# Gated and merged blocks kept on chip in the merge of a hybrid layer, x's first half loaded behind them, and longer loads in the planner's model

## The chip, the cores and the metric

The kernel runs on one core of one Trainium2 chip. The metric is the device time of one execution in microseconds (us). Three runs of the kernel before took 2212.59, 2214.92 and 2218.59 us; the median is 2214.92 us.

The core has five engines that work side by side, each on its own list of instructions in order: TensorE (PE, matrix multiplication, with its weight loads shown as PEld), VectorE (DVE), ScalarE (ACT), GpSimd (POOL) and SyncE (SP). Nearly every DMA of this kernel is issued from SP's list, so an issue that has to wait holds up every issue behind it. SBUF is the memory on the chip that the engines compute from, PSUM holds the results of matmuls until an engine reads ("evicts") them, and DRAM is outside.

## What is computed

One layer of a sequence model over 1024 positions with 1024 channels. Two branches (a gated delta rule and a gated linear attention) are computed, each is projected, and the two are merged by sigmoid gates and projected once more; then come cross attention and an MLP.

```python
y_a = o_a.reshape(bsz, seq, GDN_WIDTH) @ w_branch_gdn[i].astype(dt)
...
y_b = o_b.reshape(bsz, seq, GLA_VAL_WIDTH) @ w_branch_gla[i].astype(dt)
merged = jax.nn.sigmoid(gate_a) * y_a + jax.nn.sigmoid(gate_b) * y_b
x = x + merged @ w_out[i].astype(dt)
```

The change is in these lines: what happens to the gated `y_b` and to the merged blocks between the matmuls.

## The kernel before, in words

**Precision and tiles.** All activations are kept with the channel on the 128 partitions: a block is 128 channels by 512 positions (`HALF`), 256 KB; D = 1024 gives 8 blocks of two halves. Every float32 matrix is split in a high and a low part (`split`: ScalarE copies the rounded high part, L574, VectorE or GpSimd subtracts it from the original for the low part, L575), and a product is three matmuls (`mm3`: high by high L534, high by low L536, low by high L538).

**Seven products.** The projections use a Strassen-Winograd scheme (`wino`): one pair of output blocks (index `u`) needs seven products p = 0 to 6 instead of eight, each of four steps of three matmuls, so 12 matmuls of 512 columns. The weights for the products are sums of the raw weights (L1634 to L1639, which the planner may give to VectorE or to GpSimd), split afterwards into `wop` tiles; the raw weights are in a ring of four buffers (`RAWS`), two for each `u`. The operands of the seven products are loaded from DRAM through small staging tiles (`e` and `rawa`) and split into seven slots named A1a, A1b, B0a, B0b, B1a, B1b and t4. Each product is evicted by VectorE additions in `sums` (L1681); a block of the output is final after p = 1, 4, 5 or 6, and `done` is then called for it.

**The merge** (`phase_merge`, L1761 to L1854). It does 4 passes of `wino` with two `u` each: "yb" for the pairs (0, 1) and (2, 3), then "ya" for the same pairs. Each pass is 7 products by 2 `u` by 12 = 168 matmuls, 672 in all.

- In yb, each final half block is gated by one VectorE instruction (L1792: tanh part plus 1, times the block) and stored to DRAM tiles `m1d` (L1793): 16 stores.
- In ya, each final half block is gated (L1823), the gated half block of yb is loaded back from `m1d` and added (L1824). For the first pair the sum goes to the DRAM tiles `md` (L1829, 8 stores) and is loaded back when slots for it are free, through the staging tiles. The merged blocks are then split (`put`): high parts into B0a and B1a, low parts into B0b and B1b, for the first and second half of the positions.
- The gates come through a ring of eight half blocks in the slot A0b (`fetcher`), loaded from `tgd`; in ya the ring carries the gates and `m1d` in turn. The ring of ya is a new tile in the same slot: its first load waits until VectorE has read the last gate of yb.
- The slot A0a takes the first half of x at the start of ya, and A0b the second half at the end; `phase_out` adds x to the output projection there (L1891). `phase_out` starts its first matmuls with the merged blocks 0 to 4 and 6, then 5 and 7, of the first half.

**What sets the order.** The kernel is traced once without an order. A planner (`Plan`) reads the instructions, gives each one a cost, works out what depends on what, gives every instruction other than a matmul a latest start from the matmuls that need it (`latest`), and runs a list scheduler four times (`forward`); the best order is then fixed for every engine. The same pass decides which of the free sums go to GpSimd. A load counts in the model as landing a fixed time after its issue plus its bytes over a rate, 2050 ns and 390 bytes per ns. Any change of these numbers can therefore move instructions anywhere in the program. Buffers are given out in a ring: a load waits until the last reader of the tile that had its buffer is done.

## Time and profile before

One execution was profiled; it took 2218.4 us, its span from the first to the last instruction is 2216.6 us. It is one execution, 3.5 us above the median of the three runs, so differences are worked out within it and then taken from the median.

| what | value |
|---|---|
| median of three runs | 2214.92 us |
| profiled execution, span | 2218.4 us, 2216.6 us |
| TensorE busy | 2160.5 us, 97% of the span |
| VectorE busy | 1702.1 us, 77% |
| ScalarE busy | 1092.8 us, 49% |
| GpSimd busy | 208.2 us, 9% |
| mean granted TensorE clock | 0.991 of full |
| moved by DMA | 300.20 MB |

How to read it: a busy share is an average over stages with different limits, so the stage that the change touches has to be looked at by itself, with the stretches of time that the windows view gives. Rows of the timeline give the start, the duration, the engine, the line, the output and the inputs, and in brackets how long the engine had been idle and what released it. Matmuls overlap: a row of a matmul lasts 0.39 us at full clock though the next one starts 0.23 us later, and a VectorE row of 0.68 us is followed by the next after 0.60 us.

### The profile page before, as it was taken

The page shows a single profiled execution, that of the slowest core. Times are in us where ns is not written, and L with a number is a line of the kernel's source. Part 1 is how long each engine was busy: PE and PEld are TensorE (multiplying, and loading weights), DVE is VectorE, ACT ScalarE, POOL GpSimd, SP SyncE. Part 2 cuts the span into 40 slices and gives each one's busy share as a digit, 9 for nine tenths or more (in the row PEclk, how much of TensorE's full clock was granted, in tenths as well). Part 3 has the DMA queues.
Part 4 walks back from the last instruction along what each step waited for, and adds up shares of the span by engine and source line. Part 5 has one row for each costly group of instructions (what it writes and reads, how often), then busy time and mean ns, then how long its engine had stood idle before and what let it go on. Part 6 is the DMA issues. An engine that isn't in the chain of part 4 may idle for free.

```text
span 2216.6 us, 32151 instructions
## 1 busy us (share of the span) xinstructions
PE 2160.5 (97%) x11504; PEld 1835.2 (83%) x11504; DVE 1702.1 (77%) x3161; ACT 1092.8 (49%) x2215; POOL 208.2 (9%) x242
## 2 busy tenths in 40 slices
PE   8899999999999999999999999999999999999996
PEld 8788878988889888888878778998788888887876
DVE  7776997778796978969689965479989777567666
ACT  5544555354455545555544343465655555433433
POOL 0000000010220323222110000000100000000001
PEclk9999999999999999999999999999999999999998
DMA  8842122121311112112177841255354445687752
GB/s 273 273 153 73 59 101 86 57 83 49 120 38 50 65 47 74 48 35 76 40 248 256 285 175 67 77 168 184 116 184 142 152 157 182 212 265 249 239 175 84
DMA packets 147311, 300.20 MB, mean 135 GB/s; under 512 B 15688, under 2 KB 22216, under 8 KB 147152
## 3 DMA queue, kind: packets, MB, share of 16 engines
q1 hardware_dynamic: 140352, 289.75, 39.5%
q10 hardware_dynamic: 6800, 8.42, 1.1%
q8 instruction: 90, 1.47, 0.3%
q14 instruction: 69, 0.57, 0.1%
HBM read 212.35 MB, written 85.75 MB: 134 GB/s over the span
## 4 chain that ended last, share of the span: by engine, by line
PE 71%; DMA 11%; DVE 11%; ACT 2%; issue 2%; SPq 1%; POOL 0%; DVEq 0%; ACTq 0%; POOLq 0%
PE pd L538 18%; PE pd L534 18%; PE pd L536 18%; DMA raw<-in_w_dram 3%; PE ps L534 2%; PE ps L538 2%; PE ps L536 2%; DVE wop L575 2%; PE ps L606 1%; DMA e<-ad 1%; PE ps L1327 1%; DMA Gd<-gst 1%; SPq L503 1%; DMA A0b<-tgd 1%; DMA rawa<-pd 1%
## 5 line engine op out<-in xcount | busy, mean ns | idle before, releaser
L574 ACT ACTIVATE wop<-raw 128x512 fp32r<-128x512 f32 (+1 forms) x472 | 312.6, 669 | 377.1 <-PE pd L538 174.6
L575 DVE TENSOR_TENSOR wop<-raw,wop 128x512 fp32r<-128x512 f32 (+1 forms) x435 | 309.6, 713 | 79.4 <-ACT wop L574 77.4
L1185 DVE SCALAR_TENSOR_TENSOR acc<-pd,convw,acc 128x511 f32<-128x511 f32 x144 | 106.8, 742 | 15.7 <-ACT acc L1182 15.5
L538 PE MATMUL pd<-t,wop 128*128 128x512 f32 x268 | 107.9, 402 | 0.1
L534 PE MATMUL pd<-t,wop 128*128 128x512 f32 x268 | 106.0, 395 | 1.3 <-ACT wop L574 1.3
L536 PE MATMUL pd<-t,wop 128*128 128x512 f32 x268 | 105.1, 392 | 0.0
L534 PE MATMUL pd<-B1a,wop 128*128 128x512 f32 (+1 forms) x220 | 82.9, 377 | 0.3 <-ACT wop L574 0.3
L538 PE MATMUL pd<-B1a,wop 128*128 128x512 f32 (+1 forms) x220 | 82.8, 376 | 0.1
L538 PE MATMUL pd<-A1a,wop 128*128 128x512 f32 x180 | 73.5, 409 | 2.3 <-DVE wop L575 2.3
L534 PE MATMUL pd<-A1a,wop 128*128 128x512 f32 x180 | 72.4, 402 | 2.7 <-DVE u L1723 2.0
L536 PE MATMUL pd<-A1a,wop 128*128 128x512 f32 x180 | 71.7, 399 | 0.0
L574 ACT ACTIVATE whi<-raw 128x512 fp32r<-128x512 f32 x70 | 42.0, 626 | 55.3 <-PE pd L536 50.1
L536 PE MATMUL pd<-B0b,wop 128*128 128x512 f32 x172 | 67.6, 393 | 0.9 <-DVE B0b L575 0.9
L534 PE MATMUL pd<-A1b,wop 128*128 128x512 f32 x144 | 57.8, 402 | 3.3 <-DVE u L1723 3.3
L534 PEld LDWEIGHTS pd<-t,wop 128*128 128x128 f32 x268 | 50.4, 188 | 12.7 <-ACT wop L574 2.0
L538 PEld LDWEIGHTS pd<-t,wop 128*128 128x128 f32 x268 | 50.4, 188 | 12.6 <-DVE wop L575 1.0
L536 PEld LDWEIGHTS pd<-t,wop 128*128 128x128 f32 x268 | 50.4, 188 | 11.6
L538 PE MATMUL pd<-A1b,wop 128*128 128x512 f32 x144 | 57.5, 399 | 0.1
L536 PE MATMUL pd<-B1a,wop 128*128 128x512 f32 (+1 forms) x156 | 57.3, 367 | 0.0
L536 PE MATMUL pd<-A1b,wop 128*128 128x512 f32 x144 | 56.9, 395 | 0.0
L534 PE MATMUL pd<-A0a,whi 128*128 128x512 f32 x140 | 55.6, 397 | 0.8 <-ACT whi L574 0.8
L538 PE MATMUL pd<-A1a,wlo 128*128 128x512 f32 x140 | 56.3, 402 | 0.0
(603 smaller groups left out, 6996.4 us busy)
## 6 DMA issues: line engine op xcount, KB each, us to landing
raw<-in_w_dram SPq DMA_DIRECT2D x120, 256.0 KB, 3.9
raw<-in_w_gdn_dram SPq DMA_DIRECT2D x64, 256.0 KB, 2.8
raw<-in_w_dram SPq DMA_DIRECT2D x32, 512.0 KB, 4.4
e<-ad SPq DMA_DIRECT2D x63, 256.0 KB, 4.7
ad<-q SPq DMA_DIRECT2D x45, 256.0 KB, 2.6
rawa<-ad SPq DMA_DIRECT2D x42, 256.0 KB, 4.6
A0b<-tgd SPq DMA_DIRECT2D x32, 256.0 KB, 4.9
ad<-acc SPq DMA_DIRECT2D x30, 256.0 KB, 2.3
```

The lines of the kernel that those rows point to most:

```text
L503: self.nc.sync.dma_start(dst, src)
L534: nc.tensor.matmul(out, lh, rh, start=first and i == 0, stop=False)
L536: nc.tensor.matmul(out, lh, rl, start=False, stop=False)
L538: nc.tensor.matmul(out, ll, rh, start=False, stop=last and i == n - 1)
L574: nc.scalar.activation(hi, raw, AF.Copy)
L575: (lo_eng or nc.gpsimd).tensor_tensor(lo, raw, hi.bitcast(F32), SUB)
L606: self.nc.tensor.transpose(pt[:, i * P:(i + 1) * P], s, self.ident)
L1185: nc.vector.scalar_tensor_tensor(x, pt[:, 0:HALF - d], tap, x, MUL, ADD)
L1327: nc.tensor.matmul(pt[0:96, i * n:(i + 1) * n], PF[:, v + i, 0:96], Z, start=True, stop=True)
```

## The change

1. The gated blocks of yb are no longer stored. L1792 writes its result into a tile on chip: blocks 0 to 3 in the slot A0a, blocks 4 to 7 in a new tile `m` of the same size in a pool of its own. In ya the ring carries only gates (16 loads instead of 32), and L1824 reads the block on chip. For the first pair the merged sum is written over the gated block in A0a, and `put` splits from there; the stores to `md` and the loads from it are gone.
2. Since A0a is taken, x's first half is loaded after the splits of the second half of the first pair's blocks are issued (after p = 3 of the last pass).
3. In the planner's model a load takes 2600 ns plus its bytes at 300 bytes per ns. The cost of a ScalarE instruction with a second output and of one with a broken access pattern, and that of narrow matmuls, are changed too.
4. The pool of `m` ends with the merge; the later phases are the same.

```diff
-ROUNDS, TOP, PAD, WINDOW, LOAD, HORIZON = 4, 228656, 128, 3413, 1283, 30000
+ROUNDS, TOP, PAD, WINDOW, LOAD, HORIZON, LAND, RATE = 4, 228656, 128, 3413, 1283, 30000, 2600, 300
...
-            self.dma, self.cost, self.own, self.lat = True, 60, 2050, 2050
+            self.dma, self.cost, self.own, self.lat = True, 60, LAND, LAND
...
-            elif m == 64:
+            elif max(m, size(ins_[1])) == 64:
...
-            self.cost, self.own, self.lat = d - 100 + (240 if psum(ins_[0]) else 385) * (len(outs) > 1), 130, 135
+            broken = any(len(x.ap) > 2 and any(st != x.ap[-1][0] * x.ap[-1][1] for st, _ in x.ap[-2:-1]) for x in ins_ + outs)
+            self.cost, self.own, self.lat = d - 100 + 240 * (len(outs) > 1) + 140 * broken, 130, 135
...
-                    last[j] = min(last[j], s - q.to(o, j in self.raw[i]) - q.bytes / 390)
+                    last[j] = min(last[j], s - q.to(o, j in self.raw[i]) - q.bytes / RATE)
...
-                e = free["ring"] = max(e, free["ring"]) + o.bytes / 390
+                e = free["ring"] = max(e, free["ring"]) + o.bytes / RATE
...
+        m = [self.slot("A0a", (4, T), F32), self.til(self.mp, [P, 4, T], "m")]
+        mb = lambda blk, half: m[blk // 4][:, blk % 4, hs(half)]
+
         def yb_done(u):
             def done(i, half, x):
-                nc.vector.scalar_tensor_tensor(x, get(), 1.0, x, ADD, MUL)
-                self.nc.sync.dma_start(self.m1d[2 * u + i][:, hs(half)], x)
+                nc.vector.scalar_tensor_tensor(mb(2 * u + i, half), get(), 1.0, x, ADD, MUL)
                 more()
             return done
...
-        x[0] = self.slot("A0a", (NB, HALF), F32)
-        srcs = []
-        for us in pairs:
-            for i, half in stages:
-                for u in us:
-                    srcs += [self.tgd[2 * u + i][:, hs(half)], self.m1d[2 * u + i][:, hs(half)]]
-        get, more = fetcher(srcs)
-        for k in range(0, NB, 2):
-            self.load(x[0][:, k:k + 2], a["xT"][:, k:k + 2, 0:HALF])
+        get, more = fetcher([self.tgd[2 * u + i][:, hs(half)] for us in pairs for i, half in stages for u in us])
+
+        def load_x(half):
+            x[half] = self.slot(("A0a", "A0b")[half], (NB, HALF), F32)
+            for k in range(0, NB, 2):
+                self.load(x[half][:, k:k + 2], a["xT"][:, k:k + 2, hs(half)])
...
             def done(i, half, c):
-                ta, m1 = get(), get()
-                nc.vector.scalar_tensor_tensor(c, ta, 1.0, c, ADD, MUL)
-                nc.vector.tensor_tensor(c, m1, c, ADD)
+                blk = 2 * u + i
+                nc.vector.scalar_tensor_tensor(c, get(), 1.0, c, ADD, MUL)
                 more()
-                more()
-                blk = 2 * u + i
-                if not last:
-                    nc.sync.dma_start(self.md[blk][:, half], c)
-                elif half in mT:
+                to = c if last else mb(blk, half)
+                nc.vector.tensor_tensor(to, mb(blk, half), c, ADD)
+                if last and half in mT:
                     put(blk, half, c)
-                else:
+                elif last:
                     held.append((blk, half, c))
             return done
...
-                        put(blk, half, self.staged(sp, self.md[blk][:, half]))
+                        put(blk, half, mb(blk, half))
+                    if half:
+                        load_x(0)
```

The planner makes a new order for the whole program from this. Three places of it are shown, as rows of one engine's list: line, operation, output and inputs with their numbers, and the shape. The numbers of tiles differ between the two kernels, and from L62 on a line of the change is a few lines off the line of before (L1682 is before's L1681, L1797 is L1792, L1824 is L1823, L1827 is L1824).

VectorE, near the start of yb's second pass, before. A `raw` tile is a half of one `u`'s raw weights; raw_11806 is the second half for the second `u`, and gets the buffer that raw_11322 had.

```order
L575 TENSOR_TENSOR wop_11636<-raw_11322,wop_11636 128x512
L1681 TENSOR_TENSOR q_11746<-ps_11809,q_11746 128x512
L575 TENSOR_TENSOR wop_11877<-raw_11801,wop_11877 128x512
L1635 TENSOR_TENSOR raw_11801<-raw_11801 128x4x128
L1634 TENSOR_TENSOR raw_11805<-raw_11805,raw_11806 128x4x128
```

The same place in the change, from the last reader of raw_11310, whose buffer raw_11795 gets, up to ten rows on; the first sum that reads raw_11795 (L1635 raw_11794<-raw_11794,raw_11795) comes after four more rows.

```order
L576 TENSOR_TENSOR wop_11629<-raw_11310,wop_11629 128x512
L1682 TENSOR_TENSOR u_11660<-ps_11772,u_11660 128x512
L576 TENSOR_TENSOR A1b_11553<-e_11551,A1b_11553 128x512
L1682 TENSOR_TENSOR u_11645<-pd_11754,u_11645 128x512
L1682 TENSOR_TENSOR q_11737<-ps_11798,q_11737 128x512
L1797 SCALAR_TENSOR_TENSOR A0a_11580<-A0b_11571,q_11692 128x512
L576 TENSOR_TENSOR wop_11862<-raw_11790,wop_11862 128x512
L1682 TENSOR_TENSOR q_11752<-pd_11814,q_11752 128x512
L1636 TENSOR_TENSOR raw_11790<-raw_11790 128x4x128
L576 TENSOR_TENSOR wop_11865<-raw_11794,wop_11865 128x512
```

What moved: between the last reader of the buffer and the first reader of the new load stood three rows, now there are thirteen.

GpSimd, from the last small step of the delta rule (rs_y) to its next one in `phase_out`, before: everything that GpSimd does for the merge.

```order
L565 TENSOR_TENSOR rs_y_11218<-vv_11216,mhalf_176 128x8
L575 TENSOR_TENSOR B0b_11344<-e_11342,B0b_11344 128x512
L575 TENSOR_TENSOR B0b_11344<-e_11347,B0b_11344 128x512
L575 TENSOR_TENSOR A1b_11565<-e_11563,A1b_11565 128x512
L1634 TENSOR_TENSOR raw_11801<-raw_11801,raw_11802 128x4x128
L575 TENSOR_TENSOR t_2480_12155<-e_12153,t_2480_12155 128x512
L575 TENSOR_TENSOR A1b_12261<-rawa_12259,A1b_12261 128x512
L565 TENSOR_TENSOR rs_y_13586<-n_v_13584,mhalf_176 128x4
```

The same stretch in the change:

```order
L1331 COPY NT_10181<-subPT_5308 128x4x32 x2
L566 TENSOR_TENSOR rs_y_11195<-vv_11193,mhalf_164 128x8
L566 TENSOR_TENSOR rs_y_11206<-vv_11204,mhalf_164 128x8
L576 TENSOR_TENSOR B0a_11315<-e_11326,B0a_11315 128x512
L566 TENSOR_TENSOR rs_y_13524<-n_v_13522,mhalf_164 128x4
```

What moved: six instructions of the merge stood on GpSimd, now there is one; five more are on VectorE.

VectorE at the end of the merge, before. B0b and B1b are the low parts of the merged blocks for the first and the second half; the L1681 row is the last eviction of ya.

```order
L1681 TENSOR_TENSOR u_12672<-ps_12912,u_12672 128x512
L1824 TENSOR_TENSOR u_12657<-A0b_12277,u_12657 128x512
L1823 SCALAR_TENSOR_TENSOR u_12672<-A0b_12277,u_12672 128x512
L575 TENSOR_TENSOR B1b_12793<-rawa_12806,B1a_12792 128x512
L1824 TENSOR_TENSOR u_12672<-A0b_12277,u_12672 128x512
L575 TENSOR_TENSOR B0b_12713<-u_12657,B0a_12712 128x512
L575 TENSOR_TENSOR B1b_12793<-q_12775,B1a_12792 128x512
L575 TENSOR_TENSOR B0b_12713<-u_12672,B0a_12712 128x512
L575 TENSOR_TENSOR B1b_12793<-q_12790,B1a_12792 128x512
L575 TENSOR_TENSOR B1b_12793<-acc_12823,B1a_12792 128x512
L575 TENSOR_TENSOR B1b_12793<-acc_12845,B1a_12792 128x512
```

And in the change:

```order
L1682 TENSOR_TENSOR u_12628<-ps_12849,u_12628 128x512
L576 TENSOR_TENSOR B1b_12737<-q_12734,B1a_12736 128x512
L1824 SCALAR_TENSOR_TENSOR u_12628<-A0b_12253,u_12628 128x512
L576 TENSOR_TENSOR B0b_12665<-u_12613,B0a_12664 128x512
L1827 TENSOR_TENSOR u_12628<-m_11581,u_12628 128x512
L576 TENSOR_TENSOR B1b_12737<-acc_12764,B1a_12736 128x512
L576 TENSOR_TENSOR B1b_12737<-acc_12784,B1a_12736 128x512
L576 TENSOR_TENSOR B0b_12665<-u_12628,B0a_12664 128x512
L576 TENSOR_TENSOR wop_12884<-raw_12791,wop_12884 128x512
```

What moved: the three low parts of the second half that stood behind the last B0b now stand ahead of it. From the first split of yb's weights (the wop that reads the first half of the first raw tile) to the last B0b, VectorE's list has 248 instructions before and 257 in the change.

SP's list moves too. At the start of the program the change issues three of the four loads of x's second half between the two halves of the weights for the memory's first value projection (V0); before, they stood between the halves for the second one (V1).

More of the change, by code (lines that the diff above doesn't have):

```diff
@@ L1851, in phase_merge @@
         self.drain()
-        x[1] = self.slot("A0b", (NB, HALF), F32)
-        for k in range(0, NB, 2):
-            self.load(x[1][:, k:k + 2], a["xT"][:, k:k + 2, HALF:T])
+        load_x(1)
     def sq_sum(self, sp):
@@ L2227, in run @@
         self.Ud = dt([P, 4, 2, 4, 256], "Ud")
-        self.md = [dt([P, 2, HALF], f"md{b}") for b in range(4)]
         self.obd, self.oad, self.pd, self.hd = [[dt([P, 4, HALF], f"{n}{p}") for p in range(7)]
@@ L2236, in run @@
         self.w2d = [dt([P, HALF], f"w2d{k}") for k in range(DK)]
-        self.m1d = [dt([P, T], f"m1d{k}") for k in range(NB)]
         self.consts()
@@ L2278, in run @@
             self.load_op(sp, ob, p, src, range(4))
-        with ExitStack():
+        with ExitStack() as ctx:
+            self.mp = self.pool(ctx, "m", "left")
             self.phase_merge(sp, ob)
-            self.phase_out(sp)
-            self.phase_attn(sp)
+        self.phase_out(sp)
+        self.phase_attn(sp)
         self.phase_mlp(sp)
```

## The prediction

> **What bounds the kernel now.** First the page's head: which engine is nearest to the whole span.
>
> ```profile
> span 2216.6 us, 32151 instructions
> ...
> PE 2160.5 (97%) x11504; PEld 1835.2 (83%) x11504; DVE 1702.1 (77%) x3161; ACT 1092.8 (49%) x2215; POOL 208.2 (9%) x242
> ```
>
> TensorE is busy for all but 56 us. A change that leaves the matmuls alone, as this one does, can only win back idle time of TensorE and time at a low clock. So the next view is the windows view, cut at the stage that is changed: from VectorE's first split of yb's weights to its last B0b, then the join to the output projection, then the steady stage behind it.
>
> ```profile
> 1127.88:1297.41 169.53, 163.32 (x694) 129.69 (x695) 155.85 (x249) 74.99 (x129) 7.43 (x4) 0.99 0.74 255
> ...
> 1285.53:1300.69 15.16, 10.33 (x30) 6.83 (x29) 15.16 (x26) 4.71 (x8) 0.00 (x0) 0.78 0.43 153
> ...
> 1300.70:1350.00 49.30, 49.30 (x219) 40.80 (x218) 21.32 (x32) 17.95 (x29) 0.00 (x0) 1.00 0.37 128
> ```
>
> The columns are busy time of PE, PEld, DVE, ACT and POOL with their instructions, then the granted clock, the share of the DMA engines and GB/s. In the steady stage 219 matmuls take 49.30 us, 0.225 us each. At the join 30 matmuls take 15.16 us where they need 6.75: 8.4 us are lost, VectorE is busy all the time, and the granted clock is 0.78. The timeline of TensorE shows how:
>
> ```profile
> 1291.30 0.39 PE L538 MATMUL pd<-B0a,wop 128*128 128x512 f32 x1
> 1294.52 0.80 PE L534 MATMUL pd<-B0a,wop 128*128 128x512 f32 x1 [2.82 <-ACT B0a L574]
> 1296.26 0.80 PE L536 MATMUL pd<-B0b,wop 128*128 128x512 f32 x1 [0.95 <-DVE B0b L575]
> 1296.85 0.63 PE L538 MATMUL pd<-B0a,wop 128*128 128x512 f32 x1
> 1297.28 0.63 PE L534 MATMUL pd<-B0a,wop 128*128 128x512 f32 x1
> ```
>
> TensorE has done the part of the output projection that it can do and stands for the last two merged blocks. After the gap its steps are 0.43 us instead of 0.23, until 1300.7: some 13 steps, 2.6 us. VectorE makes the last blocks late: its last two low parts start here.
>
> ```profile
> 1295.52 0.68 DVE L575 TENSOR_TENSOR B0b<-u,B0a 128x512 fp32r<-128x512 f32 x1
> 1296.73 0.68 DVE L575 TENSOR_TENSOR B0b<-u,B0a 128x512 fp32r<-128x512 f32 x1
> ```
>
> TensorE itself would have been done much earlier: 672 matmuls of yb and ya by 0.225 us are 151.2 us from 1127.9, and the 18 of the output projection that need no late block 4.1 us more, so 1283.2. The wait ends at 1296.3. That the last two blocks are 13 us late is VectorE's queue: 249 instructions in 169.5 us, and every one of them that waits delays all behind it. Its waits in that stretch:
>
> ```profile
> DVE wop L575 <- ACT wop L574: 3.5, 7, 1.2
> DVE raw L1634 <- DMA raw<-in_w_bgdn_dram: 2.6, 2, 1.5
> DVE raw L1634 <- DMA raw<-in_w_bgla_dram: 2.0, 1, 2.0
> DVE acc L1823 <- DMA A0b<-tgd: 1.9, 1, 1.9
> DVE q L1792 <- DMA A0b<-tgd: 1.6, 1, 1.6
> DVE q L1681 <- DMA m1d<-q: 1.0, 1, 1.0
> ...
> DVE u L1823 <- DMA A0b<-tgd: 0.2, 1, 0.2
> ```
>
> And three instructions are stretched, from 0.68 to 1.78 us, each while one of the four GpSimd instructions of the stretch runs (the rows of VectorE's timeline, then GpSimd's groups there):
>
> ```profile
> 1153.22 1.79 DVE L575 TENSOR_TENSOR A1b<-rawa,A1b 128x512 fp32r<-128x512 f32 x1
> ...
> 1205.47 0.68 DVE L575 TENSOR_TENSOR B1b<-e,B1b 128x512 fp32r<-128x512 f32 x1
> 1206.07 1.78 DVE L575 TENSOR_TENSOR B1b<-rawa,B1b 128x512 fp32r<-128x512 f32 x1
> ...
> 1221.65 1.77 DVE L1639 TENSOR_TENSOR raw<-raw,raw 128x512 f32<-128x512 f32 x1
> ```
>
> ```profile
> L575 POOL TENSOR_TENSOR t<-e,t 128x512 fp32r<-128x512 f32 x1 | 1.7, 1680 | 51.2 <-DVE raw L1635 51.2
> L1634 POOL TENSOR_TENSOR raw<-raw,raw 128x512 f32<-128x512 f32 x1 | 1.7, 1676 | 3.1 <-DMA raw<-in_w_bgla_dram 3.1
> L575 POOL TENSOR_TENSOR A1b<-rawa,A1b 128x512 fp32r<-128x512 f32 x1 | 1.6, 1627 | 13.9 <-ACT A1b L574 13.9
> ```
>
> So in the merge VectorE's list is the bound: its instructions one after the other (0.60 us from start to start, as 1205.47 to 1206.07) plus its waits. The change is worth what it does to that sum.
>
> **The change part by part.**
>
> *The trips to DRAM.* Gone are 16 stores and 16 loads of m1d, 8 stores and 8 loads of md, 256 KB each, 12.6 MB of what DMA moved from 1150 to 1300:
>
> ```profile
> DMA packets 18301, 37.39 MB, mean 249 GB/s; under 512 B 2010, under 2 KB 2010, under 8 KB 18291
> ...
> A0b<-tgd SPq DMA_DIRECT2D x32, 256.0 KB, 4.9
> ...
> A0b<-m1d SPq DMA_DIRECT2D x16, 256.0 KB, 5.2
> ...
> A0a<-in_xT_dram SPq DMA_DIRECT2D x1, 512.0 KB, 5.3
> ```
>
> VectorE's own work is the same: L1792 and L1824 keep their number and size and only read or write another tile on chip. What it wins is waits: 1.0 us for a staging tile still being stored (m1d<-q), and the 0.2 us behind the ring. The ring of ya carries 16 pieces instead of 32. ScalarE's waits for reloaded blocks also go; the last blocks were never among them (they come from u, not from DRAM), so I count nothing.
>
> *The first gate of ya* (1.9 us) I keep: the new ring still starts after the last gate of yb, and in both lists four rows lie between that and the first L1823, five steps or 3.0 us against a landing of 4.9. With fewer transfers around it could shrink to nothing: 0 to 1.9 us more.
>
> *The loads that VectorE met too soon.* Before, three rows stand between the reader that frees the raw buffer and the sum that needs the next load, four steps or 2.4 us; it waited 2.0 more. The change has thirteen between, 14 steps or 8.4 us, more than the 4.4 that were needed. The places in ya have 11 to 16 steps, so the 2.0 and 2.6 go; and the ring of yb is filled among yb's operand loads, so its 1.6 goes. The lower bound is nothing: loads issued earlier also queue before others.
>
> So the waits won are 1.0 + 0.2 + 2.0 + 2.6 + 1.6 = 7.4 us.
>
> *GpSimd.* None of the four instructions is left there. The three stretches go: 3 × 1.1 = 3.3 us. They come back as VectorE instructions, below.
>
> *More instructions.* VectorE's list to the last B0b grows from 248 to 257: four from GpSimd, three low parts B1b that now stand ahead of the last B0b, and two splits of B1a that stood ahead of the stretch. 9 × 0.60 = 5.4 us lost. The stretch's start I leave at 1127.9: it hangs on the landing of yb's first weights, which have the same place on SP's list. The B1b are nothing won back behind: TensorE needs them only one group of 24 matmuls later.
>
> *x's first half.* Its first two loads now start after the last split that reads A0a, in VectorE's list 29 rows, 17 us, before the first L1891, against 5.3 us to land; hidden, and the 1300–1350 row shows DMA at 0.37 and VectorE half idle. If that cover were gone the price is the 5.3 us, and four PSUM buffers stand before TensorE. On SP only w_out's loads stand behind them, read later still.
>
> *The clock.* The slow steps stay, as the gap stays: 0.
>
> *The rest of the program.* The model's numbers move instructions everywhere, the matmuls are the same. What TensorE loses elsewhere is mostly not waiting for loads that the plan placed late:
>
> ```profile
> 0.00:110.00 110.00, 94.24 (x655) 87.42 (x656) 79.29 (x140) 64.30 (x102) 5.58 (x10) 0.97 0.82 272
> ...
> PE pd L534 <- ACT mT L689: 5.4, 1, 5.4
> PE pd L534 <- ACT kv L724: 5.4, 3, 3.3
> ...
> PE pd L534 <- DVE u L1723: 5.3, 5, 2.0
> ```
>
> The first instructions, the DMA-full start and the evictions in the MLP keep their structure. I take 0 and bound it by ±5.4, the size of the one group (kv) that a shifted load could take or double.
>
> The sum: 7.4 + 3.3 − 5.4 = 5.3 us. The profiled 2218.4 us would become 2213.1; taken from the median, 2214.92 − 5.3 = 2209.6 us. The bounds of the stage: at best the wait of 13.1 us and the 2.6 us of slow clock vanish, 15.7; at worst no wait goes, 3.3 − 5.4, 2.1 us lost.
>
> On the clock, a gap of 2.82 us with one of 0.95 us behind it was enough here for steps of 0.43 us. The Trainium skill (TensorE: Matmul & The Clock Gate, Part 1: The HAM clock gate) has the half rate after an idle window of about 3.4 us; by that a gap that shrinks a little more need not cost clock at all, which would add 2.6 us: 2207.0. I go by the row.
>
> **The rivals.**
>
> *A, the forecast*, VectorE still the bound: 2206 to 2213. 45%.
>
> *B, the gap closes.* If the ring lands in time (1.9) and the gap gets too short for the clock to fall (2.6), 5.3 + 4.5 = 9.8: 2205.1; with ScalarE's 3.5 us for wop 2201.6. For it: DMA was at 0.74 in the stretch and loses a third of its bytes. Against: VectorE's row count alone, 257 × 0.60 = 154.2 us, and the 3.5 us of waits for wop on top are 157.7, more than TensorE's 155.3. 27%.
>
> *C, the waits come back.* A list in order that no longer waits at one load waits at the next: then 7.4 is replaced and the nine instructions cost 5.4 against 3.3: 2214.9 + 2.1 = 2217.0. For it: five rows at the ring. Against: 13 rows at the raw loads. 16%.
>
> *D, slower, at the start.* Three loads of x's second half (1.57 MB) now stand between the halves of V0's weights. At 272 GB/s they push the second half back 5.8 us; the row above has TensorE waiting up to 3.3 us for kv there. If that half lands only after the last product before V0 is done, from there on each microsecond counts: 5.8 us, and 2.6 us of slow clock. 5.3 − 8.4 = −3.1: 2218.0, and with C 2225. Against: the same three loads stood between V1's halves before, so the queue is as long. 12%.
>
> **How the numbers follow.** The likeliest is A, 2209.6. A measurement of this kernel tells about 0.3% from no change, 6.6 us: below 2208.3 is faster, above 2221.5 slower. A's own range lies on both sides of the first: 20 of its 45 faster. B is faster (27). C is no change but for 1, D slower in 8 of 12. Faster 47, same 44, slower 9. The range, 2199 to 2219, takes in the stage's best bound (2199.2), C, and D's lower part; outside are about one in ten, mostly of D, and what the plan may do elsewhere.
>
> **What would show it.** In the profile after: no VectorE wait of L1634 for w_bgla or w_bgdn and none of L1681 for m1d; no VectorE instruction of 1.78 us between yb's start and the join; the first L1823 still waiting for the ring. From the first split of yb's weights to the last B0b about 164 us instead of 169.5, with VectorE busy for more of it than the 0.92 of now; the last wait of TensorE for B0b still there, with steps of 0.43 us behind it. The forecast is wrong if that wait is gone (B), if the stretch is not shorter although the named waits are (C: others in their place), or if the stretch is shorter and the total is not: then some other stage lost it, and the windows of 50 us show which, the first 110 us before all (D).

## The result, and the profile after

The changed kernel took 2187.45 us (median of 4 runs, 2185.72 to 2188.55) beside 2215.36 us of the kernel before on the same chip: a ratio of 0.9873, 95% interval 0.9856 to 0.9890, so 24 to 32 us faster. The forecast was 2209.6 us, its range 2199 to 2219. The direction was right; the gain is five times the one forecast, and the time lies outside the range. All times below are medians; of the ten executions of one experiment, latency_only, one took 5904.56 us, and the median of the other nine is 2209.88 us.

The head of the page after, which answers to the one of before (2216.6 us, TensorE 2160.5 us, 97%):

```profile
span 2184.0 us, 32086 instructions
...
PE 2147.6 (98%) x11504; PEld 1833.2 (84%) x11504; DVE 1686.5 (77%) x3165; ACT 1097.3 (50%) x2215; POOL 200.2 (9%) x238
```

The same 11504 matmuls are busy 13 us less, and TensorE stands 20 us less. By the clock records of the two traces TensorE worked 23.7 us at half clock before and 10.8 after; that accounts for some 6 of the 13 us. The merge, in the windows view from VectorE's first split of yb's weights (1120.46) to its last B0b:

```profile
1120.40:1281.90 161.50, 160.43 (x702) 131.21 (x701) 155.62 (x258) 75.32 (x132) 0.00 (x0) 1.00 0.60 197
```

161.5 us instead of 169.5, 258 instructions of VectorE (one of them starts only at the end of the stretch), none of GpSimd, and a clock of 1.00. What ended VectorE's waits there:

```profile
DVE B0b L576 <- ACT B0b L575: 4.5, 2, 3.5
DVE wop L576 <- ACT wop L575: 3.4, 2, 2.2
DVE q L1824 <- DMA A0b<-tgd: 2.2, 1, 2.2
DVE A1b L576 <- ACT A1b L575: 1.5, 1, 1.5
DVE q L1682 <- PE ps L539: 0.8, 1, 0.8
```

The first row belongs to the time before the stretch (idle 0.92 us before 1112.05 and 3.55 before 1116.29). The waits for w_bgla, w_bgdn and m1d are gone; the ring of ya still has its 2.2. At the join, VectorE's last low parts and what TensorE does meanwhile (rows of the two timelines):

```profile
1278.77 0.68 DVE L576 TENSOR_TENSOR B0b<-u,B0a 128x512 fp32r<-128x512 f32 x1
...
1281.19 0.68 DVE L576 TENSOR_TENSOR B0b<-u,B0a 128x512 fp32r<-128x512 f32 x1
```

```profile
1276.44 0.40 PE L535 MATMUL pd<-B0a,wop 128*128 128x512 f32 x1
...
1281.70 0.39 PE L537 MATMUL pd<-B1b,wop 128*128 128x512 f32 x1
1281.93 0.48 PE L537 MATMUL pd<-B0b,wop 128*128 128x512 f32 x1
1282.25 0.40 PE L539 MATMUL pd<-B0a,wop 128*128 128x512 f32 x1
```

TensorE goes from ya into the output projection without a stop; the last low part holds it for some 0.1 us, and no 0.43 us steps follow. The gap of 13 us has closed.

But the merge is not the whole. The same 250 us of the MLP's down pass, before and then after:

```profile
1900.00:2150.00 250.00, 243.27 (x1042) 196.92 (x1041) 170.68 (x266) 104.83 (x181) 8.96 (x7) 0.99 0.73 233
```

```profile
1900.00:2150.00 250.00, 250.00 (x1099) 205.73 (x1099) 168.30 (x263) 100.23 (x167) 13.58 (x10) 1.00 0.67 211
```

TensorE does 57 matmuls more in the same time and never stands. To compare kernels by stage I worked out what TensorE loses: for each matmul the time to the start of the next, less the median of that time for matmuls of the same line and size, summed over a stretch. It counts waits and slow clock together. In us:

| stretch of the span | before | after |
|---|---|---|
| 0 to 200 | 21.5 | 17.8 |
| 200 to 1090 | 15.0 | 15.0 |
| 1090 to 1400, the merge | 15.2 | 0.9 |
| 1400 to 1880 | 4.1 | 0.6 |
| 1880 to 2160, the down pass | 12.3 | 0.3 |
| from 2160 | 6.6 | 8.1 |
| sum | 74.7 | 42.7 |

Of the 32.0 us that TensorE loses less (the spans differ by 32.6) 14.3 come from the merge, 15.5 from the two stretches behind it, 3.7 from the start, and the end gives 1.5 back. (The profile of before is an execution 3 us over its median, that of after one 2 us under, so the medians show 28. The start lost between 15.9 and 21.5 us in all runs below but two, with old and new numbers alike, so its 3.7 us may be chance.)

Why TensorE stood in the down pass before is seen on ScalarE, which splits the operands that are reloaded from the DRAM tiles `ad` (staged in e and rawa). Rows of its timeline there, then of TensorE's:

```profile
2030.60 0.63 ACT L574 ACTIVATE A1a<-e 128x512 fp32r<-128x512 f32 x1 [6.66 <-DMA e<-ad]
...
2035.97 0.63 ACT L574 ACTIVATE A1a<-rawa 128x512 fp32r<-128x512 f32 x1 [2.50 <-DMA rawa<-ad]
...
2040.29 0.63 ACT L574 ACTIVATE t<-rawa 128x512 fp32r<-128x512 f32 x1 [1.48 <-DMA rawa<-ad]
```

```profile
2029.66 0.50 PE L538 MATMUL ps<-B1b,wop 128*128 128x512 f32 x1 [1.06 <-DVE wop L575]
...
2040.53 0.47 PE L534 MATMUL pd<-A1a,wop 128*128 128x512 f32 x1 [1.88 <-DVE u L1723]
```

ScalarE stands at a load that has not landed; the weight splits behind it in its list are late; VectorE waits for ScalarE's high parts, and so its own low parts and evictions (L1723) are late, and TensorE waits for those. VectorE also stands for loads of its own there, the raw weights that it sums: 19.0 us from 1880 to 2160 before, 11.7 after. ScalarE's longest waits from 1880 to 2160 us, before and then after:

```profile
ACT wop L574 <- PE ps L538: 21.6, 15, 2.1
ACT B0a L574 <- DMA e<-ad: 17.3, 7, 6.1
ACT A1a L574 <- DMA e<-ad: 16.5, 6, 6.7
ACT wop L574 <- PE pd L538: 15.0, 8, 2.1
ACT A1b L574 <- DMA e<-ad: 14.8, 6, 4.7
```

```profile
ACT wop L575 <- PE pd L539: 45.7, 24, 2.2
ACT wop L575 <- PE ps L539: 26.7, 23, 2.1
ACT wop L575 <- DVE raw L2107: 23.5, 11, 3.0
ACT A1b L575 <- DMA rawa<-ad: 6.0, 4, 3.1
```

After, ScalarE mostly waits for TensorE to give a weight buffer free: it is ahead, which is where an engine that is not the bottleneck should wait. Over the whole span its waits for these reloads are 121.5 us before (62 waits) and 64.5 us after (57), summed over the rows of the view that name e or rawa from ad.

### The profile page after: what moved, and what is told of

Read it like the earlier page. It is cut to its first block, busy times and chain, and to the rows that moved or that the text cites. A ratio compares the mean times of both kernels' runs of the same rounds, so it can differ in the third digit from the quotient of the medians.

```text
span 2184.0 us, 32086 instructions
## 1 busy us (share of the span) xinstructions
PE 2147.6 (98%) x11504; PEld 1833.2 (84%) x11504; DVE 1686.5 (77%) x3165; ACT 1097.3 (50%) x2215; POOL 200.2 (9%) x238
## 4 chain that ended last, share of the span: by engine, by line
PE 85%; DVE 2%; DMA 1%; issue 0%; ACT 0%; DVEq 0%; ACTq 0%
PE pd L535 19%; PE pd L539 19%; PE pd L537 19%; PE ps L535 5%; PE ps L539 5%; PE ps L537 5%; PE ps L607 2%; PE ps L1328 1%; PE ps L1319 1%; PE ps L1368 1%; PE ps L1248 1%; PE ps L1385 1%; PE ps L1262 1%; PE ps L1060 1%; PE ps L1375 1%; PE ps L1359 1%
## 5 line engine op out<-in xcount | busy, mean ns | idle before, releaser
L1186 DVE SCALAR_TENSOR_TENSOR acc<-pd,convw,acc 128x511 f32<-128x511 f32 (+1 forms) x144 | 106.0, 740 | 17.6 <-ACT acc L1183 17.4
L537 PEld LDWEIGHTS pd<-t,wop 128*128 128x128 f32 x268 | 50.4, 188 | 11.7
L539 PE MATMUL pd<-A0b,wlo 128*128 128x512 f32 x140 | 56.4, 403 | 0.0
```

The lines of the kernel that those rows point to most:

```text
L537: nc.tensor.matmul(out, lh, rl, start=False, stop=False)
L539: nc.tensor.matmul(out, ll, rh, start=False, stop=last and i == n - 1)
L1186: nc.vector.scalar_tensor_tensor(x, pt[:, 0:HALF - d], tap, x, MUL, ADD)
```

## The experiments

Theories at the start: **M**, the merge and the loads each win in their own place; **L**, the planner's longer loads win in the merge too; **N**, any edit shuffles the order, and the time follows by chance. The change was first taken apart.

**merge_only**: the changed kernel with the old model.

```
-ROUNDS, TOP, PAD, WINDOW, LOAD, HORIZON, LAND, RATE = 4, 228656, 128, 3413, 1283, 30000, 2600, 300
+ROUNDS, TOP, PAD, WINDOW, LOAD, HORIZON, LAND, RATE = 4, 228656, 128, 3413, 1283, 30000, 2050, 390
...
-            elif max(m, size(ins_[1])) == 64:
+            elif m == 64:
...
-            self.cost, self.own, self.lat = d - 100 + 240 * (len(outs) > 1) + 140 * broken, 130, 135
+            self.cost, self.own, self.lat = d - 100 + (240 if psum(ins_[0]) else 385) * (len(outs) > 1), 130, 135
```

> The changed kernel with all of the model's numbers as they were before (loads 2050 ns and 390 bytes per ns, the old costs of ScalarE and TensorE): only the merge on chip and x's earlier first half are left of the change. Theory M (the merge and the loads each win their own place; the changed kernel lost 14 us less of TensorE's time from 1100 to 1300 us, 4 less from 1550 to 1600, 10 less behind 2000): about 2215 - 14 = 2201 us, and the waits from 1550 to 1600 and behind 2000 are still there. Theory L (the loads' numbers win in the merge too, since half of VectorE's waits there were loads that came late): 2208 to 2212 us, with the L1635 waits for w_bgla and w_bgdn still there. Theory N (the plan's order is shuffled by any edit, and the time moves with it by chance): the places outside the merge change by several us each way, so 2195 to 2225 us with no pattern.

**loads_only**: the kernel before with LAND 2600 and RATE 300 in place of 2050 and 390 at L116, L295 and L357, and nothing else.

> The kernel before with nothing but the loads' numbers of the plan's model (2600 ns and 300 bytes per ns in place of 2050 and 390); the merge keeps its trips to DRAM and the old costs of ScalarE and TensorE stay. Theory M: the waits outside the merge go (4 us from 1550 to 1600, 10 us behind 2000, 3 at the start), the merge keeps most of its gap: 2215 - 17 = 2198 us. Theory L: part of the merge's gap goes as well, 2188 to 2194 us. Theory N: anything from 2195 to 2225 us, and not the same places as in the changed kernel.

**merge_and_loads**: the changed kernel with the last two pieces of that diff, and LAND and RATE kept at 2600 and 300.

> The changed kernel without its edits of the costs of ScalarE and TensorE (the factor 140 for broken patterns, 240 for two outputs, the 80 ns for 64 columns); merge on chip and the loads' numbers stay. Theories M and L: those costs are small, 2187 us within 5. Theory N: another order, another time, 2180 to 2205 us. If the cost edits carry the gain outside the merge: about 2205 us.

**model_only**: the kernel before with LAND, RATE and the two cost edits.

> The kernel before with all edits of the plan's model (loads and costs), and the merge with its trips to DRAM. Theory M: 2187 + 14 = 2201 us, the gap before the last blocks of the merge still there. Theory L: 2190 us, the gap mostly gone. Theory N: 2190 to 2220 us.

The four ran on one chip beside the kernel before (2213.13 us). The last three columns are TensorE's loss in us in the merge, from 1400 to 1880 and from 1880 to 2160:

| kernel | median | ratio (95%) | merge | 1400 on | down pass |
|---|---|---|---|---|---|
| merge_only | 2209.69 | 0.9979 (0.9964 to 0.9993) | 6.6 | 4.4 | 10.8 |
| loads_only | 2190.45 | 0.9896 (0.9874 to 0.9918) | 4.3 | −0.3 | −0.4 |
| merge_and_loads | 2189.94 | 0.9894 (0.9869 to 0.9919) | 3.8 | 0.3 | 0.1 |
| model_only | 2189.06 | 0.9886 (0.9865 to 0.9907) | 2.5 | 0.6 | 0.1 |

Theory L has it: two numbers of the model alone win 23 us, the merge on chip alone 3.4 (1.5 to 8.0 by the interval), and once the loads' numbers are in, taking the merge on chip makes no difference that these runs can tell (2190.45 and 2189.94; 2189.06 and the full change's 2187.45). Each of the two closes most of the merge's gap by itself, so their gains there do not add. The cost edits show no gain of their own. VectorE's waits in the merge of merge_only and then of loads_only show who removed what:

```profile
DVE raw L1634 <- DMA raw<-in_w_bgla_dram: 1.8, 1, 1.8
DVE q L1681 <- PE ps L538: 1.3, 1, 1.3
DVE raw L1634 <- DMA raw<-in_w_bgdn_dram: 1.1, 1, 1.1
```

```profile
DVE wop L575 <- ACT wop L574: 2.4, 4, 0.9
DVE q L1792 <- DMA A0b<-tgd: 1.6, 1, 1.6
DVE A1b L575 <- ACT A1b L574: 0.9, 1, 0.9
DVE A1b L1875 <- ACT A1a L1892: 0.8, 1, 0.8
DVE q L1823 <- DMA A0b<-tgd: 0.4, 1, 0.4
```

With the merge alone, the loads of the raw weights are still met too soon; with the loads alone these waits are gone although all trips to DRAM are still there.

**Which number, and how steady.** Four kernels, each the kernel before with other values of LAND and RATE and no other edit. Theory P: every load is late by a fixed time (LAND). Theory Q: loads are late because they queue (RATE).

> The kernel before with one number of the model changed: a load takes 2600 ns in place of 2050; the rate stays 390 bytes per ns. Theory P (each load comes late by a fixed time, whatever else is under way): most of the 23 us that both numbers won, 2192 to 2196 us. Theory Q (loads come late because they stand behind each other, where the DMA engines are 0.7 to 0.8 busy: the merge, the last 200 us): a third at most, 2203 to 2210 us, and the waits behind 2000 us stay. Theory N (chance of the order): no link with either.

> The kernel before with one number of the model changed: 300 bytes per ns in place of 390; a load's own time stays 2050 ns. Theory Q: most of the 23 us, 2192 to 2198 us, and the waits of the merge and behind 2000 us are gone, since the busiest 100 us of the trace moved 279 GB/s at a DMA share of 0.83, about 336 at a full share, so that 390 promised more than was ever moved. Theory P: 2205 to 2210 us. If either number alone does it, any push of some 0.5 us is enough, and both runs give 2190 to 2196 us.

> The kernel before with loads longer still in the model: 3200 ns and 250 bytes per ns. If the loads are early enough with 2600 and 300 (theory of saturation: what TensorE loses then, 47 us, lies at the first and last 200 us and in dependences, not at loads): 2188 to 2192 us as with 2600 and 300. If loads were still late there: 2180 to 2186 us. If earlier loads now take buffers or the ring from others: over 2195 us.

> The kernel before with the model's load 50 ns longer, 2100 in place of 2050, and the old rate: too little to make a load of 256 KB (4.9 us to land in the trace) be on time, but enough to give another order. Theory N: the time moves by 5 to 20 us in either direction, and with it the places where TensorE waits. Theories P and Q: within 4 us of the kernel before, 2209 to 2217 us, and the waits from 1550 to 1600 and behind 2000 us still there.

Then neighbours of the old and the new numbers, before_2500_300 and before_2000_390 on the kernel before, after_2500 and after_2700 on the changed one:

> The kernel before with 2500 ns and 300 bytes per ns, one step beside the 2600 and 300 of the run with the loads' numbers alone (2190 us). Theory R (whether loads are late sets what is lost in the MLP's second half; with about 3.4 us for a load of 256 KB they are not): 2187 to 2197 us, ScalarE's waits for the reloaded halves of the down pass (e and rawa from ad) under 60 us in all where the kernel before has 121, and TensorE lost less than 2 us from 1900 to 2150 us. Theory N (2190 was a lucky order; a step of 50 ns from the old numbers cost 20 us): 2195 to 2235 us.

> The changed kernel with 2500 ns in place of 2600. Theory R: 2184 to 2194 us, no wait of TensorE from 1550 to 1600 and from 1900 to 2150 us. Theory N: as wide as 2180 to 2210 us, the waits there come back.

> The changed kernel with 2700 ns in place of 2600. Theory R: 2184 to 2194 us as with 2500. Theory N: 2180 to 2210 us. If the loss with 3200 and 250 (2229 us, 36 us of it before 200 us) grows step by step with the number, 2190 to 2195 us, with more lost in the first 200 us.

> The kernel before with 2000 ns in place of 2050 and the old rate: the other side of the run with 2100, which was 20 us slower. Theory R with chance on top: loads late as before, 2208 to 2240 us, with 4 us lost from 1550 to 1600 us and over 10 us from 1900 to 2150 us. Theory N: it could as well be 2190 us, with nothing lost at these places.

All by the numbers of the model, each ratio to the kernel before on the same chip; the last column is ScalarE's waits for e and rawa from ad over the span:

| LAND, RATE | kernel | median | ratio (95%) | merge | 1400 on | down pass | ad waits |
|---|---|---|---|---|---|---|---|
| 2000, 390 | before_2000_390 | 2241.56 | 1.0111 (1.0096 to 1.0127) | 19.6 | 10.5 | 21.6 | 163 |
| 2050, 390 | before | 2213 to 2216 | 1 | 15.2 | 4.1 | 12.3 | 121 |
| 2100, 390 | nudge | 2234.04 | 1.0092 (1.0071 to 1.0113) | 15.5 | 7.2 | 26.1 | 162 |
| 2600, 390 | latency_only | 2210.30 | 0.9980 (0.9969 to 0.9992) | 13.4 | 3.3 | 7.5 | 124 |
| 2050, 300 | rate_only | 2202.07 | 0.9945 (0.9924 to 0.9967) | 4.9 | 2.9 | 7.3 | 100 |
| 2600, 300 | loads_only | 2190.45 | 0.9896 (0.9874 to 0.9918) | 4.3 | −0.3 | −0.4 | 21 |
| 2600, 300 | the change | 2187.45 | 0.9873 (0.9856 to 0.9890) | 0.9 | 0.6 | 0.3 | 65 |
| 2500, 300 | before_2500_300 | 2193.03 | 0.9893 (0.9876 to 0.9909) | 6.0 | 0.3 | 0.0 | 38 |
| 2500, 300 | after_2500 | 2195.81 | 0.9910 (0.9895 to 0.9925) | 2.6 | 1.0 | 0.0 | 26 |
| 2700, 300 | after_2700 | 2185.61 | 0.9865 (0.9851 to 0.9880) | 0.4 | −0.1 | 0.3 | 19 |
| 3200, 250 | still_longer | 2228.64 | 1.0066 (1.0043 to 1.0089) | 18.5 | 2.1 | 4.2 | 23 |

Theories P and Q both fall short: either number alone wins 4 or 12 us, both together 23. Theory N is right about the old numbers: a step of 50 ns either way costs 20 to 25 us. It is wrong about the new ones: all that lie at 2500 to 2700 and 300, with and without the merge and the cost edits, took 2186 to 2196 us and lost next to nothing in the MLP. So this is a floor with its own small chance on it, not one lucky order. Some luck was on the other side: of the three orders planned with 2000, 2050 and 2100 at 390 the kernel before is the fastest, so beside its neighbours the change would have won more. (after_2500 is 2 us above its forecast; it lost 24 us from 200 to 1090, where the others lose 15 to 17. before_2000_390 is 1.6 us above its own.) The nudge's down pass, to set beside the two rows of before and after:

```profile
1900.00:2150.00 250.00, 237.19 (x983) 185.96 (x983) 162.34 (x251) 101.20 (x176) 9.30 (x7) 0.97 0.70 228
```

And longer is not simply better: with 3200 and 250 the reloads are hardly waited for, but 36.4 us are lost before 200 us and 18.5 in the merge. The first 200 us of still_longer, then of the changed kernel, and in still_longer TensorE's gap at the join:

```profile
0.00:200.00 200.00, 171.85 (x992) 150.84 (x993) 131.02 (x213) 97.91 (x156) 11.79 (x14) 0.95 0.61 204
```

```profile
0.00:200.00 200.00, 187.00 (x1073) 164.43 (x1074) 139.85 (x228) 104.09 (x163) 11.09 (x14) 0.97 0.64 213
```

```profile
1311.71 0.80 PE L534 MATMUL pd<-B0a,wop 128*128 128x512 f32 x1 [6.97 <-DVE B0b L575]
```

**Is it the lateness, or an order that is bad for another reason?** The next two keep the order of the kernel before on every engine: the order is planned with the full program and then applied to one whose transfers are smaller. Three quarters of these operands are left out, and the instructions behind them read the loaded quarter four times over.

quarter_reloads (quarter_trips does the same to the stores and loads of m1d and md):

```
-    def staged(self, sp, src, both=True):
+    def staged(self, sp, src, both=True, cols=HALF):
...
+        if self.made and cols < HALF:
+            self.load(raw[:, 0:cols], src[:, 0:cols])
+            return raw[:, 0:cols]
         self.load(raw, src)
...
-                self.split(self.staged(sp, self.ad[k // 4][p][:, k % 4]), t[:, 0, j], t[:, 1, j], nc.vector)
+                self.split(self.staged(sp, self.ad[k // 4][p][:, k % 4], cols=128), t[:, 0, j], t[:, 1, j], nc.vector)
```

> The kernel before with its order of instructions kept word for word on all engines, but the 105 reloads of ad in the MLP's down pass (e and rawa from ad) move a quarter of their bytes: 128 columns of each half row, which the splits behind them read four times over, so that the down pass computes with the first quarter of its operands and the output is not the layer's. Theory R (late loads cost the time, not the order as such): the same order with loads that land sooner loses less; of the 12 us that TensorE loses from 1880 to 2160 us at least half goes, 2205 to 2209 us, and ScalarE's 121 us of waits for these tiles fall under 80. Theory N (the order of the instructions as such costs it): no change, 2214 within 2 us.

> The kernel before with its order kept word for word, but the trips of the merge (m1d and md, stores and loads) move a quarter of their bytes: 128 columns of each, read four times over behind the load, so that the gated sums are wrong. Work and order of every engine stay. If the trips cost time through the bytes they move (the loads of w_bgla and w_bgdn stand behind them): VectorE's waits of 4.6 us for these two and the rest of its DMA waits go, the merge loses 5 to 8 us less, 2206 to 2210 us. If they cost it through their places in the lists (what is behind what): no change, 2214 within 2 us.

quarter_reloads took 2208.32 us beside 2213.66, ratio 0.9971 (0.9962 to 0.9981). The issues of the raw weights and of these tiles, before and then here, and the down pass here:

```profile
raw<-in_w_dram SPq DMA_DIRECT2D x120, 256.0 KB, 3.9
...
e<-ad SPq DMA_DIRECT2D x63, 256.0 KB, 4.7
...
rawa<-ad SPq DMA_DIRECT2D x42, 256.0 KB, 4.6
```

```profile
raw<-in_w_dram SPq DMA_DIRECT2D x120, 256.0 KB, 2.9
...
e<-ad SPq DMA_DIRECT2D x63, 64.0 KB, 2.9
...
rawa<-ad SPq DMA_DIRECT2D x42, 64.0 KB, 2.9
```

```profile
1900.00:2150.00 250.00, 249.77 (x1093) 204.80 (x1092) 173.83 (x269) 106.99 (x185) 9.51 (x7) 1.00 0.54 170
```

With the same order, loads that land 1.8 us sooner take the loss of the down pass to 0.6 us and the waits for them from 121.5 to 9.2 us. That is shown: the loss in the down pass is the loads' lateness, not the order. Which loads is less sure. The smaller reloads also take the DMA share from 0.73 to 0.54, and the raw weights, whose bytes are as before, land 1.0 us sooner; VectorE's waits for them from 1880 to 2160 us fall from 19.0 to 2.5 us. How much of the loss belongs to the reloads and how much to the weights was not taken apart. The medians differ by 5.3 us, the two profiles by 11.7 in the down pass: the profile of before is one of its longer executions, and what a usual one loses there no profile shows.

quarter_trips took 2207.77 us, ratio 0.9971 (0.9960 to 0.9983), 6 us less. But the waits that I had put down to the trips' bytes did not go:

```profile
DVE raw L1645 <- DMA raw<-in_w_bgdn_dram: 2.3, 2, 1.1
DVE raw L1645 <- DMA raw<-in_w_bgla_dram: 2.0, 1, 2.0
DVE acc L1836 <- DMA A0b<-tgd: 1.3, 1, 1.3
```

They were 2.6, 2.0 and 1.9 (the line numbers are shifted by the added code). The merge's loss fell from 15.2 to 10.5; the down pass, in which nothing is changed, fell from 12.3 to 6.9. So one profile of an order with late loads seems good to about 5 us in such a stage, and where the 6 us of quarter_trips come from is left open.

**Which use of the numbers.** The planner uses a load's length twice: in `forward`, where it says when the reader may be placed, and in `latest`, where it ranks the load among what SP could issue. One at a time, on the kernel before:

```
-                    last[j] = min(last[j], s - q.to(o, j in self.raw[i]) - q.bytes / RATE)
+                    last[j] = min(last[j], s - q.to(o, j in self.raw[i]) + (LAND - 2050) * q.dma - q.bytes / 390)
```

That is longer_in_flow, against loads_only; longer_in_due has LAND = 2050 and 390 in `forward`, and takes 550 more and RATE = 300 in this line.

> The kernel before with the longer loads (2600 ns, 300 bytes per ns) only in the part of the planner that goes forward in time and says when what a load brings can be used; the due times by which it ranks what is ready keep 2050 and 390. If the gain is that no engine is put to wait at a load that has not landed, since other work is placed ahead of its reader: 2190 to 2196 us. If it is that loads are asked for earlier (due times): 2208 to 2216 us.

> The same with the two parts changed about: due times with 2600 ns and 300 bytes per ns, the forward part with 2050 and 390. If loads asked for earlier are the gain: 2190 to 2200 us. If the readers placed behind other work are: 2208 to 2235 us, with TensorE losing 10 us or more from 1880 to 2160 us.

longer_in_flow: 2191.41 us beside 2213.66, ratio 0.9897 (0.9878 to 0.9915), all of the gain. longer_in_due: 2241.19 us, ratio 1.0119 (1.0099 to 1.0139), 28 us slower, and 6 us above its forecast. Their down passes in this order:

```profile
1900.00:2150.00 250.00, 250.00 (x1096) 205.55 (x1095) 171.27 (x270) 104.69 (x175) 10.67 (x8) 1.00 0.70 224
```

```profile
1900.00:2150.00 250.00, 240.39 (x1020) 191.16 (x1019) 161.50 (x253) 102.41 (x178) 5.40 (x5) 0.99 0.73 231
```

So the gain is not a load that is ranked earlier; it is that its reader is placed behind other work that can run meanwhile. The traces agree: from the issue of an e reload to the start of its split on ScalarE it is 4.8 us before and 4.7 in longer_in_flow (median of 63), the same distance, but before ScalarE stands idle in it, and in longer_in_flow, as in the kernel after, it first waits for TensorE:

```profile
ACT wop L574 <- PE pd L538: 41.9, 26, 2.1
ACT wop L574 <- DVE raw L2109: 26.2, 12, 3.2
ACT wop L574 <- PE ps L538: 23.3, 20, 2.1
ACT B0b L574 <- DMA rawa<-ad: 6.9, 5, 2.5
```

The last two ask whether the due times do harm, in the changed kernel and with the 3200 and 250 of still_longer:

> The changed kernel with the longer loads only in the planner's forward part (2600 ns, 300 bytes per ns) and the old numbers (2050, 390) in its due times: the way that won all of the gain in the kernel before. If longer due times do harm by themselves (27 us in the run that had them alone), this beats the changed kernel: 2178 to 2184 us. If they do so only where the forward part has the short loads: 2184 to 2192 us, no difference to the changed kernel's 2187.

> The kernel before with 3200 ns and 250 bytes per ns in the forward part alone and the old numbers in the due times; with them in both it took 2229 us. If the due times did that harm: 2186 to 2196 us, and under 25 us lost before 200 us. If the forward part did it (readers placed so late that the work behind them is late): 2220 to 2232 us, with some 36 us lost before 200 us.

after_longer_in_flow: 2193.10 us beside 2215.37, ratio 0.9899 (0.9882 to 0.9916), 1 us above its forecast; not better than the change, so no harm of the long due times is seen where the flow has long loads too. still_longer_in_flow: 2239.20 us, ratio 1.0106 (1.0083 to 1.0129), 7 us above its forecast, with 32.7 us lost before 200 us and 21.1 in the merge: the harm of 3200 and 250 is in the forward part. That readers placed too late hold up the work behind them fits this, but no run took that chain apart.

No kernel beat the change beyond doubt: after_2700 is 2 us lower, within the intervals.

## Why the prediction was wrong

**The step that failed** is "The rest of the program. The model's numbers move instructions everywhere, the matmuls are the same. … I take 0 and bound it by ±5.4". By the profiles 17.7 of the 32.0 us lie outside the merge, and the longer loads alone won 23 us. The bound came from the size of one wait of TensorE, kv, at the start. It should have come from what hangs on loads: the three largest rows of ScalarE's waits for e from ad in the down pass are 48.6 us, VectorE's waits for raw weights there 19.0, and TensorE lost 12.3 us behind them. On the other side it had no bound of that kind at all: steps of 50 ns cost 20 to 25 us. That "the evictions in the MLP keep their structure" was true of their number and beside the point; what stands ahead of them had moved. (What TensorE lost from 1400 to 1880, 4.1 us, is 1.0 or less in all seven kernels with 2500 to 2700 and 300 in both parts of the planner, and 1.4 and 3.3 in the two that have them in the flow alone; no run took that wait apart.)

**The merge** went by rival B, and further, though not by B's first reason, since the ring still did not land in time. The parts:

- VectorE's list: the 257 instructions of the order ran; no stretched one of 1.78 us and no wait for m1d, as forecast.
- The waits for w_bgla and w_bgdn (4.6 us) went, but not by the merge's order, as I had read: with the merge alone 1.8 and 1.1 are left, and with the longer loads alone none.
- The first gate of ya: forecast to wait 1.9, it waits 2.2.
- The stretch: 164 us forecast, 161.5 measured, so 8.0 less than before instead of 5.3. VectorE's idle time fell from 13.7 to 5.9 us (169.53 less 155.85, 161.50 less 155.62), 7.8 us against the 7.4 forecast. Its busy time fell by 0.2 us, where three stretches less and nine instructions more were to add 2.1; what made the other instructions 2.3 us shorter is open.
- "The stretch's start I leave at 1127.9" failed. Before, TensorE waited 2.56 us for the first split weights of yb and started with them; after, they were split at 1120.46 and TensorE came at 1121.58. So VectorE starts 1.1 us ahead.
- TensorE's own end was mis-sized. It takes 160.4 us from its first matmul of yb to the one that needs the last low part, where I had 155.3: its pace in the stretch is 0.228 us from start to start, not 0.225 (2.4 us over 690 matmuls; the steady row has 0.227 between starts too, and 49.30 by 219 counted matmuls that the edges of the window cut), six more matmuls of the output projection need no late block (1.4 us), and it waits 1.1 us for A1a in yb.

8.0, 1.1 and 5.1 us are 14.2, more than the wait of 13.1; so it closed, and the slow clock went with it. Of the stage's best bound, 15.7 us, 14.3 came. The sentence on the clock gate in the Trainium skill was not put to the test by the changed kernel, since no gap was left there. The trace of before tells against reading it as a stop of 3.4 us: behind the stop of 1.88 us at 2040.53, shown above, the windows view has a clock of 0.50 from 2041.50 to 2044.80, with steps of 0.43 us. So a gap that shrinks a little more can still cost clock, and here the measurement decides.

**The rivals.** A was forecast at 45% and did not happen: VectorE and TensorE reach the join together. C, other waits in their place, is refuted for the merge. D, the start slower by 8.4 us, is refuted: it lost 17.8 us instead of 21.5. merge_only's 2209.69 us, beside the 2209.6 forecast for the whole, is no proof of the working: its profile has the waits for raw weights still there and the wait at the join nearly gone all the same.

## What to carry to other kernels

Where a planner orders in-order lists, a number in its model is part of the kernel: bound an edit of it by every wait in the trace that such a number could have put there, on the engines one step behind TensorE too, and by a step to either side of the old value. Look at what the engines that feed the bottleneck wait for: if it is loads, the order is fragile, and it should be mostly for the bottleneck to free a buffer. How long a load should be in the model is found by trying a few values: for the reloads of 256 KB, which landed in 4.7 us, 2.7 us (2050 ns and 256 KB at 390) was too short, 3.4 to 3.6 us (2500 to 2700 and 300) right in all seven kernels and 4.2 us (3200 and 250) too long in both of its two, and it is the part of the planner that places the reader which needs it.

## What the runs showed of the hardware

Reloads of 64 KB landed in 2.9 us where those of 256 KB took 4.7, with the same order; a line through both would meet no bytes at 2.3 us. That is near the fixed time of about 2 us that the Trainium skill gives (DMA: Bandwidth & Descriptors, Anatomy of one DMA; its figure is for transfers that GpSimd issues, and these are SP's). The further 0.6 us that its rate of 436 GB/s would add for 256 KB is an estimate from that page; the row has 2.4, at a DMA share of 0.73.

But the size is not all that differs between the two rows. In quarter_reloads the raw weights, 256 KB each, landed in 2.9 us as well, where they had taken 3.9 before, and the DMA share of the down pass was 0.54 instead of 0.73. So the line is no price per byte: in one and the same kernel 256 KB landed as soon as 64 KB, and what the rows show is that loads of unchanged size land sooner when others move fewer bytes.

Whether a kernel with late loads is less steady in itself is not shown: merge_only's runs lie between 2202.64 and 2213.83 us (10 runs), those of loads_only between 2189.32 and 2194.01 (4 runs), but the four of still_longer_in_flow, in which hardly a reload is late, spread as widely (2236.70 to 2240.96) as those of loads_only.
